# Reordered head pairs, batched value products and a TensorE-held residual in a two-layer streaming encoder step

## The chip, the cores and the metric

The kernel runs on one core of one Trainium2 chip. The metric is the device time of one execution in microseconds (us), from the first to the last instruction of the core plus what lies around them. TensorE appears in the profile as two engines: PE (matmuls) and PEld (loading of the stationary 128 x 128 weights). DVE is VectorE, ACT is ScalarE, POOL is GpSimd, and SP issues most of the DMA transfers.

## The reference, cut to what matters

One inference step of an encoder of two layers, width 1024, over T = 1088 tokens: 1024 new frames of one stream ("prompt") and 64 frames of a running stream ("sample"). All is float32. Layer 0 is a Mamba-2 mixer and a SwiGLU FFN, layer 1 a banded attention and a SwiGLU FFN. The part that the change touches most:

```python
def rmsnorm(x, w):
    return x * lax.rsqrt(jnp.mean(x * x, axis=-1, keepdims=True) + EPS) * w
...
# layer 1: K and V from the residual x, 16 heads of 64
kv = rmsnorm(x, kv_norm_w) @ w_kv
q  = rmsnorm(x, nw[0]) @ attn_w_q
# queries in chunks of 64; a chunk sees itself and the 8 chunks before it
s = einsum('bqhd,bkhd->bhqk', q, k) * 64 ** -0.5 + rel_bias[:, clip(qpos - kpos, -256, 256) + 256]
p = softmax(where(valid, s, -inf))
m = einsum('bhqk,bkhd->bqhd', p, v) @ attn_w_o
# both layers
x = x + rmsnorm(m, nw[1])
x = x + rmsnorm(swiglu(rmsnorm(x, nw[2]), ffn_w_in, ffn_w_out), nw[3])
```

In layer 0, `m` comes from a projection, a causal convolution of four taps with SiLU, a chunked state-space scan and an output projection. K and V of the last 512 prompt tokens and of the sample are outputs too. Sample queries see 512 cached rows of K and V beside their own.

## The kernel before, in words

**Tiling.** Activations lie transposed, 128 features on partitions and tokens along the free axis. The tokens are cut in three *slices* `SL` of 384, 384 and 320, and, where FFN pairs and the output of the attention are concerned, in four quarters `QS` of 256, 256, 288 and 288. For accuracy each matmul operand is split into a high and a low part, and each product is made of three (L415 to L417: high x high, high x low, low x high, in `passes`). One projection *unit* for a slice is 8 x 3 = 24 matmuls into one PSUM bank (`mm`, two banks).

**Order.** TensorE runs in an order written out by hand: the main program issues units, and side tasks are Python generators in a `Stream` (L73). Each matmul adds an estimate of its time to `st.t`; a task yields (cost, delay, condition) and is resumed by `pump` once `st.t` has reached its due time and its condition holds; `wait_for` advances `st.t` by 0.25 a step until its condition is true. All of this happens when the program is built. The chip then runs each engine's queue in order, with semaphores between the engines. The other engines' order follows priorities (`tc.high_priority`; HIP = 3000).

**Weights.** `Weights` (L200) is a ring in the order given by `plan`: a raw buffer (two) filled by a 512 KB DMA on SP's queue (`load`, L224), then `plain` (L243), which makes the high part on ACT (L312) and the low part on DVE (L313) into one of three `hl` buffers. The attention's weights are first scaled on POOL by a norm's weights (L248).

**Layer 0.** The convolution (L716 to L748) takes a projection out of PSUM into `raw`, makes the first tap on ACT (L738) into the tile `cvt` (one buffer), adds three taps on DVE (L740) and applies SiLU on ACT (L744 to L747) into `dst`. L992 sends the low parts of the first weights to POOL (`W.eng = G`). The FFN's first product runs pair by pair (`run_pair`, L1219); the FFN's output projection (L1391 to L1425, matmuls L1405 to L1407) goes slice by slice, with the `end` task (L1311) of each slice behind it: it takes the sum of squares through `rstd` (L443, matmuls L448), broadcasts the reciprocal root (`rb_steps`), multiplies the output by it (L1326 or L1323) and adds the residual x (L1324, L1327). In layer 0 it then makes the split operands `u` for layer 1 and a second sum of squares (L1352), whose broadcast `rb` (`done2` holds ("rb", s)) is multiplied into K, Q and V when they leave PSUM. In layer 1 the last slice's end is the kernel's tail: multiplies on DVE and, for m = 1, 3, 5, on POOL, adds on DVE, one output DMA for each m.

**Attention (L1452 to L1749).** Heads go in pairs j = 0 to 7, one pair to 128 partitions. `evk` (L1506), `evq` (L1526) and `evv` (L1558) take a unit of K, Q or V out of PSUM. `evk` keeps high and low of each head stacked on 128 partitions; `evq` makes for each head `qh` twice (two ACT copies, L1537 and L1538) and `ql` twice (DVE, L1540), so that one product with `qh` and one with `ql` give all terms. `evv` spawns `v_task` (L1545, transposes V) and three `att_task` (L1575), one for each block of 128 queries. A block has three stages, A, B and C, counted in `cur`:

- A: scores of both heads into a tile `S` of two banks (L1610, L1611), then on DVE bias and maximum (L1617), combination of the two banks' maxima (L1622), negation (L1623), on ACT the exponential (L1624), on DVE reciprocal (L1625) and scaling (L1626).
- B: up to five transposes for each head (L1638) into a tile of the same two buffers (`psS`), copies to `pT` on DVE or ACT (L1642, L1644; four buffers).
- C: `pT` with V (L1661, weights 64 wide) into `po`, one of two banks of `ax`, kept through the three blocks of a slice; then a copy `ot` (L1668) and a DMA (L1669) to the DRAM tensor `oscr`.

Block b + 1 may start A once block b - 1 has made B, and B once its own A's scores are due and C of block b - 2 is done. `build_o` (L1681) reads `oscr` back quarter by quarter (L1688) and splits it (L1689, L1690) for the output projection.

The main order (L1700 to L1749): V, K, Q of pair 0 for slices 0 and 1; K of pair 1 for these; a wait for slice 2's norm, ("rb", 2); pair 0's slice 2 as K, Q, V; then for each pair j = 1 to 7 and each slice K, Q, V, each behind a wait that keeps the ring of K and V tiles (`KBUF` = 5, `free_k`, L1676) and of Q tiles (three) from being overrun. The side load of cached K and V rows (`load_side`, L1477) stands in that loop behind a wait for the pair before to be done.

## Time and profile before

Three runs took 3090.6, 3090.92 and 3097.8 us. One more was profiled; where the profile is read below, it is this one.

| what | us |
|---|---|
| median of three runs | 3090.92 |
| the profiled execution's own time | 3083.24 |
| its span, first to last instruction | 3081.1 |
| stretch 0 to 1610 us (layer 0, to near the end of its FFN's output projection) | 1610.0 |
| stretch 1610 to 1700 (the rest of it, first K, V and Q units, slice 2's norm) | 90.0 |
| stretch 1700 to 1792 (first attention blocks) | 92.0 |
| stretch 1792 to 2194.65 (six steady head pairs) | 402.65 |
| stretch 2194.65 to 3081.1 (last pair, output projection, FFN of layer 1) | 886.45 |

The mean clock that TensorE was granted is 0.990 of full speed. The span holds 329 MB of DMA traffic, 107 GB/s on average.

A page of the profile lists for each engine its busy time; groups of instructions by source line ("L313 DVE ..."), with count, busy time, mean length and the idle time ahead of them; and what released an engine from a wait (in the view of the waits a row names the waiting engine and line, "<-" the engine and line that ended the wait, then the idle us in all, the number of waits and the longest). A timeline row has start, duration, engine, line, operation, output <- input, shape and count, and in brackets the idle time ahead of it and its releaser. Matmul durations overlap, since they are pipelined: the pace is read from start to start. A row of the windows view has the stretch, its length, busy time and instruction count of PE, PEld, DVE, ACT and POOL, the granted clock, the DMA engines' share and GB/s.

### The profile page before, as it was taken

How to read it: one execution, taken by the hardware profiler on the slowest of the kernel's cores; microseconds unless marked ns; L12 is line 12 of the kernel's file. 1: busy time of each engine (PE TensorE's matmuls, PEld its weight loads, DVE VectorE, ACT ScalarE, POOL GpSimd, SP SyncE). 2: the span in 40 equal slices, each digit the busy share in tenths (PEclk: the TensorE clock that was granted, in tenths of full speed). 3: DMA queues.
4: the chain of work that ended last, by engine and by line, in shares of the span. 5: the costliest groups of instructions: out<-in, count | busy, mean ns of one | idle time of the engine just before them, and what ended most of it. 6: DMA issues, size and time to landing. Idle time of an engine off the chain costs nothing.

```text
span 3081.1 us, 56781 instructions
## 1 busy us (share of the span) xinstructions
PE 2989.6 (97%) x21761; PEld 2908.2 (94%) x21761; DVE 2117.1 (69%) x4579; ACT 1419.9 (46%) x2512; POOL 880.4 (29%) x1011
## 2 busy tenths in 40 slices
PE   8999999999999999999999899999999999999998
PEld 8899999999999999999999788889898999999997
DVE  8878788796778545574566788887768645575544
ACT  6656565664443222344443454444554332244432
POOL 2333333331344343341223111100054334342112
PEclk9999999999999999999999999999999999999999
DMA  3111111125553222345663121122355222246654
GB/s 118 39 52 51 57 51 59 51 89 151 170 166 107 83 78 74 99 149 176 194 188 123 61 68 60 55 61 62 114 168 166 78 78 76 79 124 183 205 181 132
DMA packets 176511, 329.14 MB, mean 107 GB/s; under 512 B 17360, under 2 KB 124752, under 8 KB 176240
## 3 DMA queue, kind: packets, MB, share of 16 engines
q1 hardware_dynamic: 174448, 319.16, 33.4%
q0 software_dynamic: 1792, 6.36, 1.1%
q8 instruction: 171, 2.80, 0.4%
q14 instruction: 100, 0.82, 0.1%
HBM read 262.85 MB, written 62.60 MB: 106 GB/s over the span
## 4 chain that ended last, share of the span: by engine, by line
PE 81%; DVE 10%; DMA 3%; issue 2%; ACT 2%; POOL 2%; SPq 0%; DVEq 0%; POOLq 0%; ACTq 0%
PE mm L415 8%; PE px L1235 8%; PE px L1236 8%; PE px L1237 8%; PE mm L417 8%; PE mm L416 8%; PE po L1407 5%; PE po L1405 5%; PE po L1406 5%; PE mmx L415 2%; PE mmx L416 2%; PE mmx L417 2%; PE po L1661 2%; PE ptp L1638 2%; DVE hl L313 1%
## 5 line engine op out<-in xcount | busy, mean ns | idle before, releaser
L313 DVE TENSOR_TENSOR hl<-raw,hl 128x1024 fp32r<-128x1024 f32 (+1 forms) x292 | 359.7, 1233 | 313.5 <-ACT hl L312 312.9
L415 PE MATMUL mm<-r,hl 128*128 128x384 f32 (+2 forms) x1664 | 560.3, 337 | 5.9 <-ACT BT L746 4.8
L417 PE MATMUL mm<-r,hl 128*128 128x384 f32 (+2 forms) x1664 | 540.2, 325 | 0.6 <-DVE hl L313 0.6
L416 PE MATMUL mm<-r,hl 128*128 128x384 f32 (+2 forms) x1664 | 539.8, 324 | 0.0
L312 ACT CAST hl<-raw 128x1024 fp32r<-128x1024 f32 (+1 forms) x295 | 297.8, 1014 | 302.1 <-PE po L1407 98.7
L1236 PE MATMUL px<-r,hl 128*128 128x288 f32 (+1 forms) x1192 | 350.1, 294 | 0.0
L415 PEld LDWEIGHTS mm<-r,hl 128*128 128x128 f32 x1664 | 316.2, 190 | 14.6 <-issue 6.7
L441 POOL TENSOR_TENSOR ssum<-ssum,sq 128x256 f32<-128x256 f32 (+3 forms) x153 | 166.0, 1091 | 540.8 <-ACT sq L440 537.6
L416 PEld LDWEIGHTS mm<-r,hl 128*128 128x128 f32 x1664 | 316.5, 190 | 0.4
L417 PEld LDWEIGHTS mm<-r,hl 128*128 128x128 f32 x1664 | 315.6, 190 | 1.0 <-DVE hl L313 1.0
L1235 PE MATMUL px<-r,hl 128*128 128x288 f32 x1056 | 311.7, 295 | 4.1 <-DVE u L1250 3.9
L1237 PE MATMUL px<-r,hl 128*128 128x288 f32 x1056 | 311.2, 295 | 0.0
L1237 PE MATMUL px<-rx,hl 128*128 128x256 f32 x816 | 229.1, 281 | 6.5 <-DVE hl L313 6.5
L1235 PE MATMUL px<-rx,hl 128*128 128x256 f32 x816 | 230.0, 282 | 0.0
L1236 PEld LDWEIGHTS px<-r,hl 128*128 128x128 f32 x1192 | 224.0, 188 | 0.1
L1406 PE MATMUL po<-rx,hl 128*128 128x384 f32 (+1 forms) x640 | 208.0, 325 | 0.0
L1235 PEld LDWEIGHTS px<-r,hl 128*128 128x128 f32 x1056 | 198.7, 188 | 5.7 <-DVE u L1250 5.7
L1405 PE MATMUL po<-rx,hl 128*128 128x384 f32 (+1 forms) x608 | 199.6, 328 | 0.0
L1237 PEld LDWEIGHTS px<-r,hl 128*128 128x128 f32 x1056 | 198.4, 188 | 0.0
L1407 PE MATMUL po<-rx,hl 128*128 128x384 f32 (+1 forms) x608 | 198.0, 326 | 0.3 <-DVE hl L313 0.3
L1236 PE MATMUL px<-rx,hl 128*128 128x256 f32 x680 | 191.1, 281 | 0.0
L262 POOL TENSOR_TENSOR tt<-raw 128x512 f32<-128x512 f32 x44 | 60.0, 1363 | 396.9 <-DMA raw<-in_w_f_dram 207.8
(348 smaller groups left out, 8147.4 us busy)
## 6 DMA issues: line engine op xcount, KB each, us to landing
raw<-in_w_f_dram SPq DMA_DIRECT2D x204, 512.0 KB, 3.8
raw<-in_w_in_dram SPq DMA_DIRECT2D x40, 512.0 KB, 3.6
raw<-in_w_f_dram SPq DMA_DIRECT2D x48, 384.0 KB, 3.2
sg<-hscr SPq DMA_DIRECT2D x88, 192.0 KB, 3.6
raw<-in_w_so_dram SPq DMA_DIRECT2D x32, 512.0 KB, 3.9
raw<-in_w_kv_dram SPq DMA_DIRECT2D x18, 512.0 KB, 3.6
raw<-in_w_o_dram SPq DMA_DIRECT2D x16, 512.0 KB, 3.8
sg<-hscr SPq DMA_DIRECT2D x44, 160.0 KB, 3.6
```

The source lines that it names most:

```text
L312: self.nc.scalar.copy(h, v)
L313: (eng or self.eng or self.nc.vector).tensor_tensor(lo, v, h, op=ALU.subtract)
L415: PE.matmul(ps[:, :n], h_, xh, start=(first and i == 0), stop=False)
L416: PE.matmul(ps[:, :n], h_, xl, start=False, stop=False)
L417: PE.matmul(ps[:, :n], l_, xh, start=False, stop=(last and i == nk - 1))
L441: (eng or G).tensor_tensor(ssum[:, :n], ssum[:, :n], q[:, :n], op=ALU.add)
L1235: PE.matmul(ps, wh, ah[:, k, :], start=(k == 0), stop=False)
L1236: PE.matmul(ps, wh, al[:, k, :], start=False, stop=False)
L1237: PE.matmul(ps, wl, ah[:, k, :], start=False, stop=(k == 3))
L1405: PE.matmul(ps[:, :n], wh, xh, start=(k == 0), stop=False)
L1406: PE.matmul(ps[:, :n], wh, xl, start=False, stop=False)
L1407: PE.matmul(ps[:, :n], wl, xh, start=False, stop=(k == FT - 1))
```

## The change

The edits, in the order of the diff:

1. Scaled weights (attention): eight scaled ACT copies and eight DVE multiply-subtracts of 128 x 128 in place of POOL's scaling, ACT's cast and DVE's subtraction (`scaled`).
2. `rstd` with two sums keeps them in separate PSUM columns and adds them on DVE.
3. The convolution works in `dst`; the tile `cvt` is gone. `W.eng = G` is gone.
4. The tail: x goes into PSUM on TensorE (product with the identity) for m = 0 to 5, DVE multiplies y, TensorE adds it to x in PSUM, and ACT copies the sum out; m = 6 and 7 are added on DVE. Some due times change.
5. The second norm of layer 0's last slice is issued once K's product for slice 2 has been ("k2").
6. During the FFN output projections the weight splits have priority 1500 (`W.pri`).
7. Attention order: for each pair and slice K, V, Q instead of K, Q, V; `att_task` is spawned by `evq`, 5.0 behind it, and `v_task` 3.0 behind `evv`. The side load is a task of its own. All three evacuations have priority 3000. Q tiles have two buffers.
8. `ql`'s second copy comes from the first by a DMA within SBUF on SP's queue.
9. The softmax computes the negative scores' minimum, chained from the first bank to the second, so that combination and negation go; it and the copies of B have priority 1000.
10. C is held: `values` runs a slice's three blocks together ahead of the first transposes of the next slice (for the last pair, behind its own slice's last block). `pT` has six buffers.
11. The last pair's outputs of slices 0 and 1 stay on chip for `build_o`, which reads three pairs rather than four from DRAM for that half.
12. Around slice 2 of pair 0: the products of K and V are issued ahead of the wait for ("rb", 2), and their evacuations behind it; then V of pair 1 for slices 0 and 1, then Q of pair 0 for slice 2.

```diff
-EP_W, ER_W, EQ_W = (9.4, 9.4, 5.0), (8.9, 8.9, 4.5), (11.0, 11.0, 11.0)
+EP_W, ER_W, EQ_W = (9.4, 9.4, 2.2), (8.9, 8.9, 3.3), (11.0, 11.0)
-LDP, ENP = 1500, (0, 0, 1500)
+LDP, ENP, ATP = 1500, (0, 0, 1500), 1000
...
         if it.get("kscale") is not None:
-            v3 = r.rearrange("p (k m) -> p k m", m=P)
-            self.nc.gpsimd.tensor_tensor(v3, v3, it["kscale"].unsqueeze(2).to_broadcast([P, KD, P]), op=ALU.mult)
-        self.part(it, "w", None, r[:, :n])
+            self.scaled(it, r)
+        else:
+            self.part(it, "w", None, r[:, :n])
...
+    def scaled(self, it, r):
+
+        self.used.append(self.hl)
+        t = self.hl.get()
+        for k in range(KD):
+            sl, c = slice(k * P, (k + 1) * P), it["kscale"][:, k:k + 1]
+            self.nc.scalar.activation(t[:, 0, sl], r[:, sl], AF.Copy, scale=c)
+        for k in range(KD):
+            sl, c = slice(k * P, (k + 1) * P), it["kscale"][:, k:k + 1]
+            self.nc.vector.scalar_tensor_tensor(t[:, 1, sl], r[:, sl], c, t[:, 0, sl], op0=ALU.mult, op1=ALU.subtract)
+        it["w"] = t[:, 0, :], t[:, 1, :]
...
-        for i in range(nb):
-            for j, t in enumerate(ts):
-                PE.matmul(
-                    sp[:, i:i + 1], t[:, i * P:(i + 1) * P], ones[:, 0:1], start=(j == 0), stop=(j == len(ts) - 1)
-                )
+        for j, t in enumerate(ts):
+            for i in range(nb):
+                c = 4 * j + i
+                PE.matmul(sp[:, c:c + 1], t[:, i * P:(i + 1) * P], ones[:, 0:1], start=True, stop=True)
...
+            if more is not None:
+                V.scalar_tensor_tensor(a, sp[:, 4:4 + nb], inv, a, op0=ALU.mult, op1=ALU.add)
...
-                cvt = sb2.tile([P, 384], F32, tag="cvt", bufs=1, name="cvt")
+
                 cw = C_CW + ct * 4
-                A.activation(cvt[:, :w_], raw[:, 0:w_], AF.Identity, bias=col(C_CB + ct), scale=col(cw))
+                A.activation(dst[:, :w_], raw[:, 0:w_], AF.Identity, bias=col(C_CB + ct), scale=col(cw))
                 for k in range(1, 4):
                     V.scalar_tensor_tensor(
-                        cvt[:, :w_], raw[:, k:k + w_], col(cw + k), cvt[:, :w_], op0=ALU.mult, op1=ALU.add
+                        dst[:, :w_], raw[:, k:k + w_], col(cw + k), dst[:, :w_], op0=ALU.mult, op1=ALU.add
                     )
                 if s < 2:
-                    A.activation(dst[:, :384], cvt[:, :384], AF.Silu)
+                    A.activation(dst[:, :384], dst[:, :384], AF.Silu)
                 else:
-                    A.activation(dst[:, 0:256], cvt[:, :256], AF.Silu)
-                    A.activation(dst[:, 256:320], cvt[:, 259:323], AF.Silu)
+                    A.activation(dst[:, 0:256], dst[:, :256], AF.Silu)
+                    A.activation(dst[:, 256:320], dst[:, 259:323], AF.Silu)
...
-        W.eng = G
...
+                if s == 2 and more is None:
+                    yield 0, EP_W[2]
+                steps = rb_steps(ss, n, out, ER_W[s], more=more)
...
+                    xps = {}
+                    def hold(ms):
+                        for m in ms:
+                            xps[m] = mm("xp") if m > 3 else px.tile([P, 512], F32, tag="mm", name="xp")
+                            PE.matmul(xps[m][:, :n], ident, xs[m][0], start=True, stop=False)
+
+                    yield next(steps)
+                    hold(range(4))
+                    yield next(steps)
+                    yield next(steps)
+                    hold((4, 5))
+                    for m in range(KD):
+                        ym = y[:, m, :n]
+                        V.scalar_tensor_tensor(ym, ym, col(cpost2 + m), out[0], op0=ALU.mult, op1=ALU.mult)
+                        if m in xps:
+                            PE.matmul(xps[m][:, :n], ident, ym, start=False, stop=True)
+                            A.copy(ym, xps[m][:, :n])
+                        else:
+                            V.tensor_tensor(ym, ym, xs[m][0], op=ALU.add)
+                        nc.sync.dma_start(xout[:, m, o:o + n], ym)
...
-                yield 0, EQ_W[s]
+                yield (0, EQ_W[s]) if s < 2 else (0, 0, lambda: "k2" in done2)
...
+            W.pri = LDP
...
-    W.plan(W_V[0], W_K[0], W_Q[0], W_K[1], W_V[0])
-    for j in range(1, 8):
-        W.plan(W_K[j], W_Q[j], W_V[j])
+    W.plan(W_V[0], W_K[0], W_Q[0], W_K[1], W_V[0], W_V[1], W_K[1], W_Q[1])
+    for j in range(2, 8):
+        W.plan(W_K[j], W_V[j], W_Q[j])
...
+        def side_task(j):
+
+            yield 0, 0, lambda: cur["C"] >= 9 * j
+            load_side(j)
...
-                Q = [[sb2.tile([P, 384], F32R, tag=f"Q{x}{e}", bufs=3, name=f"Q{x}{e}") for x in "hl"] for e in range(2)]
+                Q = [[sb2.tile([P, 384], F32R, tag=f"Q{x}{e}", bufs=2, name=f"Q{x}{e}") for x in "hl"] for e in range(2)]
...
-                    for x in range(2):
-                        V.tensor_tensor(ql[H2[x], :n], qf[H2[e], :n], qh[H2[e], :n], op=ALU.subtract)
+                    V.tensor_tensor(ql[H2[e], :n], qf[H2[e], :n], qh[H2[e], :n], op=ALU.subtract)
+                    nc.sync.dma_start(ql[H2[1 - e], :n].bitcast(F32), ql[H2[e], :n].bitcast(F32))
+                for i in range(3):
+                    st.spawn(att_task(j, 3 * s + i), 5.0 + 0.1 * i)
...
-                st.spawn(v_task(j, s, vt), 1.5 if j else 5.0)
-                for i in range(3):
-                    st.spawn(att_task(j, 3 * s + i), 2.0 + 0.1 * i)
+                st.spawn(v_task(j, s, vt), 3.0 if j else 5.0)
...
+            yield 0, 0, lambda: (
+                late and cur["A"] == seqn and cur["B"] >= seqn - 1 and st.t >= cur["t"] and s in d["K"] and s in d["Q"] and (b < 8 or "Ck" in d)
+            )
...
+                low = TOP
+                with tc.high_priority(ATP):
+                    for pi, (f0, f1) in enumerate([(0, split)] + ([(split, w_)] if split < w_ else [])):
+                        V.tensor_tensor_reduce(
+                            out=sc[:L, f0:f1], in0=sp[:L, pi, :f1 - f0], in1=brev[:, f0:f1],
+                            scale=-1.0, scalar=low, op0=ALU.add, op1=ALU.min, accum_out=mx[:L, pi:pi + 1],
+                        )
+                        low = mx[:L, pi:pi + 1]
+                    A.activation(sc[:L, :w_], sc[:L, :w_], AF.Exp, bias=low, scale=-1.0, accum_out=mx[:L, 3:4])
+                    V.reciprocal(mx[:L, 3:4], mx[:L, 3:4])
+                    V.tensor_scalar(sc[:L, :w_], sc[:L, :w_], mx[:L, 3:4], None, op0=ALU.mult)
...
-            yield 1.1 * w_ / 640, AT_W1, lambda: cur["B"] == seqn and cur["C"] >= seqn - 1 and st.t >= cur["t"]
+            yield 1.1 * w_ / 640, AT_W1, lambda: (
+                cur["B"] == seqn and st.t >= cur["t"] and (i > 0 or not held or held[0][:2] in v_done)
+            )
+            cost = values(held) if i == 0 else 0
...
-                pT = late["sb3"].tile([P, 5, P], F32, tag="pT", bufs=4, name="pT")
+                pT = late["sb3"].tile([P, 5, P], F32, tag="pT", bufs=6, name="pT")
...
+            held.append((j, s, i, L, nkt, w_, k0, PTs))
+            yield cost, 0
+            if (j, s) == (7, 2) or (j == 7 and i == 2):
+                yield 0, AT_W2, lambda: (j, s) in v_done
+                yield values(held), 0
+        def values(blocks):
...
+            while blocks:
+                j, s, i, L, nkt, w_, k0, PTs = blocks.pop(0)
+                d = kqv[j]
...
+                    ot = late["sb1"].tile([P, 384], F32, tag=f"o7{s}" if j == 7 and s < 2 else "ot", name="ot")
+                    with tc.high_priority(HIP if j == 7 else 0):
+                        A.copy(ot[:, :n], po[:, :n])
+                    nc.sync.dma_start(od_[:, j, o:o + n], ot[:, :n])
+                    if j == 7 and s < 2:
+                        last_o[s] = ot
+                    att_done.append((j, s))
+                cur["C"] += 1
...
+        def free_q(q, stage):
 
             j_, s_ = divmod(q - KBUF, 3)
-            return j_ < 0 or cur["C"] > 9 * j_ + (6, 7, 8)[s_]
+            return j_ < 0 or cur[stage] > 9 * j_ + (6, 7, 8)[s_]
 
...
+                    nk = 4 - (kh and q < 2)
...
+                if nk == 3:
+                    yield 0, 0, lambda: all((7, s) in att_done for s in of)
+                    for s in of:
+                        a, b = max(o, SL[s][0]), min(o + n, SL[s][0] + SL[s][1])
+                        src = last_o[s][:, a - SL[s][0]:b - SL[s][0]]
+                        with tc.high_priority(HIP):
+                            A.copy(h[:, 3, a - o:b - o], src)
+                            V.tensor_tensor(l_[:, 3, a - o:b - o], src, h[:, 3, a - o:b - o], op=ALU.subtract)
...
-        st.wait_for(lambda: ("rb", 2) in done)
...
+        wv = W.get()
+        n2, kv2 = SL[2][1], []
+        for w in (wk, wv):
+            ps = mm("mm")
+            passes(ps, w, lambda k: u[2][k], [(k, k) for k in range(KD)], n2, parts=4)
+            kv2.append(ps)
+            done.append("k2")
+            st.pump()
+        st.wait_for(lambda: ("rb", 2) in done)
+        for ps, e in zip(kv2, (evk, evv)):
+            e(0)(2, ps)
             W.put()
+            st.pump()
+        wv = W.get()
+        units(wv, 1, evv, (0, 1))
+        st.wait_for(lambda: cur["A"] >= 3)
+        units(wq, 0, evq, (2,))
+        W.put()
         for j in range(1, 8):
             if j > 1:
                 load_pair(j)
             load_bias(j)
...
+            ws = [W.get(), W.get() if j > 1 else wv, W.get()]
+            evs = [evk, evv, evq]
+            for s, i in [(s, i) for s in range(NSL) for i in range(3) if j > 1 or s == 2 or i == 2]:
+                q = 3 * j + s
+                if (s, i) == (2, 0):
+                    st.spawn(side_task(j))
+                st.wait_for(lambda: cur["A"] >= 3 * (q - 1) if i == 2 else free_q(q, "AC"[i]))
+                units(ws[i], j, evs[i], (s,))
...
+        st.wait_for(lambda: cur["C"] == 8 * NCH and 1 in uo)
```

130 lines of the change are left out of this document (51 added, 79 removed).

## The prediction, made before the result was known

> **What bounds the kernel now.** I read the page's busy times first, then the stretches of the windows view, then who waited for whom inside a stretch, and last the timeline at the waits.
>
> ```profile
> span 3081.1 us, 56781 instructions
> ...
> PE 2989.6 (97%) x21761; PEld 2908.2 (94%) x21761; DVE 2117.1 (69%) x4579; ACT 1419.9 (46%) x2512; POOL 880.4 (29%) x1011
> ```
>
> TensorE is busy for 2989.6 of 3081.1 us, and the change takes none of its products away. Only 91.5 us of idle time, the time at a low clock, and what TensorE loses between kinds of matmul can be won. Where the idle time lies (columns: length, then busy us with instruction counts of PE, PEld, DVE, ACT, POOL, the granted clock, DMA share, GB/s):
>
> ```profile
> 0.00:150.00 150.00, 134.77 (x864) 124.59 (x864) 123.69 (x305) 96.62 (x166) 40.83 (x89) 0.98 0.23 77
> 1595.00:1610.00 15.00, 11.48 (x57) 10.95 (x57) 11.10 (x10) 8.65 (x16) 10.10 (x8) 0.77 0.61 190
> 1672.00:1693.00 21.00, 14.64 (x70) 14.07 (x70) 16.45 (x32) 7.87 (x17) 6.07 (x10) 0.76 0.30 96
> 1700.00:1792.00 92.00, 81.34 (x610) 72.43 (x609) 75.61 (x237) 45.18 (x103) 13.99 (x11) 0.96 0.20 63
> 1792.00:2194.65 402.65, 386.18 (x2998) 356.14 (x2998) 322.46 (x1001) 195.88 (x435) 29.68 (x35) 1.00 0.20 62
> 1763.53:1766.94 3.41, 1.57 (x11) 1.08 (x10) 2.02 (x4) 2.70 (x5) 0.00 (x0) 1.00 0.02 9
> 1766.94:1770.35 3.41, 2.95 (x12) 2.76 (x13) 3.28 (x13) 2.06 (x6) 0.00 (x0) 0.50 0.15 50
> 3063.00:3081.10 18.10, 3.96 (x22) 2.85 (x20) 10.05 (x23) 0.86 (x2) 2.99 (x3) 0.62 0.21 72
> ```
>
> Idle time in these: start 15.2 us; end of layer 0's FFN 3.5; slice 2's norm ahead of the attention 6.4; first attention blocks 10.7; the six steady head pairs 16.5; the tail 14.1. That is 66 of the 91.5 us, all in places that the change touches. A wait costs more than itself: from 1763.53 PE worked 1.57 of 3.41 us, and the next 3.41 us had a clock of 0.50.
>
> **Part by part.** *AV products by slice.* Each block's AV product (L1661) is its own batch, 8 pairs x 9 blocks = 72. The change holds them and runs a slice's three together, 24 batches.
>
> ```profile
> 1848.66 0.34 PE L1610 MATMUL S<-K,Qh 128*128 128x384 f32 x1
> 1848.84 0.33 PE L1611 MATMUL S<-K,Ql 128*128 128x384 f32 x1
> 1849.10 1.09 PE L1661 MATMUL po<-pT,Vn 128*64 128x128 f32 x16
> 1850.13 0.42 PE L415 MATMUL mm<-r,hl 128*128 128x320 f32 x1
> 1850.38 0.31 PE L416 MATMUL mm<-r,hl 128*128 128x320 f32 x1
> 1850.53 0.31 PE L417 MATMUL mm<-r,hl 128*128 128x320 f32 x1
> ```
>
> From start to start a 384-column product takes 0.18 us; ahead of the AV batch (its weights are 64 wide) it takes 0.26: 0.08 lost. A 320-column product takes 0.15, so 128 columns take 0.06; 16 make 0.94, and 1.03 pass: 0.09 lost. The first projection after it takes 0.25 in place of 0.15: 0.10 lost. So 0.27 us a batch, times 48 batches fewer, **-13**. Where only transposes follow, less is lost: 0.15 or 7 us is my low end. The weight loader's own idle time ahead of these batches bounds it above:
>
> ```profile
> PEld po L1661 <- issue: 8.8, 35, 0.3
> ```
>
> 8.8/35 = 0.25 us on the way in and no more than that out: 0.5 x 48 = 24 us.
>
> *The steady pairs' waits.*
>
> ```profile
> PE ptp L1638 <- DVE mx L1617: 9.8, 6, 2.6
> PE S L1610 <- ACT pT L1642: 5.9, 6, 1.0
> ```
>
> ```profile
> 1847.65 0.15 DVE L1625 RECIPROCAL mx<-mx 128x1 f32<-128x1 f32 x1
> 1847.73 0.46 DVE L1540 TENSOR_TENSOR Ql<-qf,Qh 64x320 fp32r<-64x320 f32 x1
> ...
> 1848.66 3.10 DVE L1540 TENSOR_TENSOR Ql<-qf,Qh 64x320 fp32r<-64x320 f32 x3
> ```
>
> ```profile
> 1845.35 2.03 POOL L248 TENSOR_TENSOR raw<-raw,pcs 128x1024 f32<-128x1024 f32 x1 [32.05 <-DMA raw<-in_w_kv_dram]
> 1849.42 1.99 POOL L248 TENSOR_TENSOR raw<-raw,pcs 128x1024 f32<-128x1024 f32 x1 [2.04 <-DMA raw<-in_w_kv_dram]
> ```
>
> ```profile
> 1852.74 1.44 PE L1638 MATMUL ptp<-ident,sc 128*128 128x128 f32 x8 [1.47 <-DVE mx L1617]
> ```
>
> One Ql split takes 0.46 us alone; three take 3.10 while POOL scales a weight. The score reductions behind them in DVE's queue come late, both score buffers stay full, and PE waits 1.47 us for one. The change takes L248 off POOL, halves the Ql splits (six of 0.46, 2.8 us a pair), drops two kinds of 128x1 operation (18 negations and ten maxima a pair, at the 0.15 of the reciprocal: 4 us), and puts the softmax at priority 1000, ahead of weight splits. It adds eight multiply-subtracts of 128x128 in place of one subtraction:
>
> ```profile
> L313 DVE TENSOR_TENSOR hl<-raw,hl 128x1024 fp32r<-128x1024 f32 x18 | 22.0, 1223 | 3.3 <-ACT hl L312 3.1
> ```
>
> ```profile
> 23.40 0.29 DVE L990 TENSOR_TENSOR dtw<-dtr,dtw 128x128 fp32r<-128x128 f32 x1
> ```
>
> ```profile
> 1705.98 0.25 ACT L1642 COPY pT<-ptp 128x128 f32<-128x128 f32 x1
> ```
>
> 8 x 0.29 = 2.3 us against 1.22, three weights a pair: +3.3 us on DVE; eight casts of 0.25 = 2.0 us on ACT where one of about 1 us stood. Net, DVE loses some 3.5 us of work a pair and all the time behind POOL; ACT (49% busy) gains 3. Both lie beside TensorE: a weight buffer is refilled while the pair's other units and blocks run, so this costs nothing unless a refill comes over 10 us late. Of the 15.7 us I take **-12**; the ends are 0 and -16.5. A longer hold of the pT tiles is covered by six buffers for four, and `po` no longer keeps one of the two `ax` banks through three blocks. Moving the side load out of the main loop lets it wait without holding the units behind it.
>
> *Ql's second half by DMA.* This is the added wait. evq now issues two transfers of 96 KB for each slice on SP's queue, each waiting there for its DVE split; weight loads and K/V outputs queue behind for that time, and these have slack. The scores wait for the landing. No row shows a transfer within SBUF; the nearest are
>
> ```profile
> hscr<-u SPq DMA_DIRECT2D x34, 128.0 KB, 1.7
> ```
>
> ```profile
> cr<-in_ckT_dram SPq DMA_DIRECT2D x16, 128.0 KB, 2.6
> ```
>
> Head 1's path after its unit: multiply, three casts and a split on 64 partitions at about 0.46-0.5 each, 2.4 us with idle engines, then 1.7 to 2.6: 4.1 to 5.0 us, with DVE 80% and ACT 49% busy around it. Its first scores are placed 5.0 us of counted work behind evq. So PE waits between 0 and 1.1 us for each of 24 slices if the engines are prompt, and up to 3 if they are not. I take 0.3: **+7** (ends 0 and +72).
>
> *Slice 2's products beside its norm.*
>
> ```profile
> PE nst L448 <- POOL ssum L1352: 4.0, 1, 4.0
> PE nst L448 <- DVE ssum L1352: 2.4, 1, 2.4
> ```
>
> The norm's sums are now placed behind K's slice 2, so the unfinished Q and K units and that product come first; V's 3.5 us (24 x 0.15) cover the chain behind the sums, and two V units of pair 1 follow. The 6.4 us idle and up to 0.24 x 14.6 = 3.5 us of low clock can go; about 2 stays where the broadcast waits for DVE: **-7.5** (ends -3 and -9.9).
>
> *Weight splits at priority 1500 in the output projections.*
>
> ```profile
> PE po L1405 <- ACT hl L312: 2.5, 1, 2.5
> PE po L1407 <- DVE hl L313: 1.0, 1, 1.0
> ```
>
> 3.5 us idle and 0.23 x 11.5 = 2.6 of low clock. POOL's squares still slow DVE there: **-4** (ends 0 and -6).
>
> *First attention blocks.* The 10.7 us have the same causes as the steady waits, but V of pair 1 has moved ahead, so fewer projection pieces lie between the blocks: **-4** (ends +6 and -12).
>
> *Start.* The weight split on POOL and the single cvt tile go.
>
> ```profile
> PE mm L415 <- ACT BT L746: 4.8, 1, 4.8
> ```
>
> The split comes back on DVE at 1.2 us each, so part of this: **-3** (ends 0 and -7).
>
> *Tail.*
>
> ```profile
> 3070.09 4.30 DVE L1326 SCALAR_TENSOR_TENSOR y<-y,pcs,rb 128x320 f32<-128x320 f32 x5 [1.98 <-ACT rb L479]
> 3074.32 1.00 DVE L1324 SCALAR_TENSOR_TENSOR y<-y,pcs,r 128x320 f32<-128x320 f32 x2
> 3075.24 2.08 DVE L1327 TENSOR_TENSOR y<-y,r 128x320 f32<-128x320 f32 x5
> 3077.25 0.54 DVE L1324 SCALAR_TENSOR_TENSOR y<-y,pcs,r 128x320 f32<-128x320 f32 x1
> ```
>
> 7.7 us of DVE, the first five at 0.86 beside POOL. After: eight multiplies and two adds at 0.42 = 4.2; the other adds go through TensorE and ACT beside them, with a last copy behind: **-3** (ends 0 and -4.5). The last pair's outputs kept on chip skip a DRAM trip; its wait is in the 15.7 us, and I count nothing more.
>
> Sum: -13 -12 +7 -7.5 -4 -4 -3 -3 = -39.5. The profiled execution took 3083.24 us (span 3081.1), so it would take 3044; the runs shown have a median of 3090.92, 7.7 above it, so I forecast **3051**.
>
> One rule of the Trainium skill speaks against part of this. "TensorE: Matmul & The Clock Gate", section "What's actually happening", has the clock fall to half after at least one idle window of about 3.4 us. Read strictly, waits of 1.8 to 2.5 us would cost no clock, 5 us of the clock terms would not be there, and the sum would be -34.5, 3056. The trace disagrees: the window with 1.57 us of work in 3.41 was followed by 0.50.
>
> **The rivals.** (1) *All waits go.* The ql transfer is in time (-7), the steady waits vanish (-4.5), the first blocks and the small terms reach their ends (-15): 3025. For it: all steady waits end at DVE or ACT work that POOL delays. (2) *The attention keeps its waits.* With PE's order fixed at build time, new places wait where old ones went: +16 on the forecast, 3067. For it: DVE stays above 70% busy, and the score buffers remain two. (3) *ql comes late* (slower than before). The mechanism is the transfer behind head 1's split. Without it the change is worth 46.5 us; 46.5/24 = 1.9 us a slice breaks even, about 3090. At 3 us a slice it costs 72, and as the clock falls after such waits, some 4-5 us more in all: about 3120. For it: DVE's and ACT's queues were 80% and 49% busy, and a split is seen to take 3.10 for three. Against it: POOL's L248 was what stretched it.
>
> **How the numbers follow.** Forecast 3051 (3037 to 3062): 0.46. Rival 1: 0.22. Rival 2: 0.19. Rival 3 near break-even: 0.05; well past it: 0.08. The range 3020 to 3079 leaves out the last two. Faster by over 0.3% (9.3 us; about what a measurement of this kernel tells from no change) is 0.46 + 0.22 + 0.19 = 0.87, same 0.05, slower 0.08.
>
> **What would show it.** Steady pairs of about 63 us in place of 67.1 (402.65/6), 24 stretches of L1661 rather than 72; no wait for the score buffers of over 1 us in them; at the start of a slice a wait of S for ql of under 0.5 us; PE idle under 3 us in slice 2's norm, with the clock at 1.00; the multiplies of the tail at 0.42 each. The forecast is wrong if S waits 1 us or more for ql's landing in most slices, or if weights of the attention come late because their sixteen small operations have no priority.

## The result, and the profile after

The changed kernel took 3046.7 us (median of four runs, 3044.14 to 3050.39) beside 3091.86 for the kernel before: a ratio of 0.9853, 95% interval 0.9837 to 0.9868, or 45 us less. A second measurement, beside runs of before of its own, gave 0.9859 (0.9842 to 0.9876). The forecast was 3051. The profiled execution took 3046.85, its span is 3045.2. That is 35.9 us under the span of the profile of before, and not 45, since the profiled execution of before (3083.24) was faster than its median.

Page of the changed kernel: span and busy times.

```profile
span 3045.2 us, 56936 instructions
...
PE 2981.5 (98%) x21785; PEld 2913.9 (96%) x21785; DVE 2075.4 (68%) x4498; ACT 1463.6 (48%) x2703; POOL 816.2 (27%) x975
```

TensorE's idle time fell from 91.5 to 63.7 us and its busy time by 8.1; switching between kinds of matmul and time at a low clock show as busy time, so what they gave lies in the second number. To see where, both traces are cut at the starts of TensorE instructions that both kernels have (the last cut is at an end): the first product `yo` of the state-space scan, the first FFN product `px` of layer 1, the first and last output-projection product `po` of both FFNs, and the last value product of the attention. Each stretch up to the tail holds the same number of matmuls in both. (The second profile is that of `changed_again` below.)

| stretch, us | before | changed | changed, second profile |
|---|---|---|---|
| start to first `yo` | 98.60 | 103.15 | 105.50 |
| to first `po` of layer 0 | 1273.94 | 1274.80 | 1275.20 |
| to last `po` of layer 0 | 273.62 | 269.39 | 269.15 |
| to last value product (the attention) | 568.78 | 528.08 | 527.47 |
| to first `px` of layer 1 | 164.37 | 169.80 | 165.03 |
| to first `po` of layer 1 | 419.69 | 421.72 | 420.40 |
| to last `po` of layer 1 | 265.13 | 264.84 | 264.68 |
| to the end (tail) | 17.00 | 13.38 | 13.39 |

The attention gave 41 us, the first output projection 4, the tail 3.6; the start got 4.6 to 6.9 longer. The 5.4 us lost behind the attention in the first profile were that execution's: the second has 0.7.

Windows of the changed kernel (length, busy us and counts of PE, PEld, DVE, ACT, POOL, clock, DMA share, GB/s): the first attention blocks and five further pairs.

```profile
1687.43:1800.37 112.94, 108.48 (x855) 102.45 (x854) 90.86 (x300) 70.15 (x180) 0.65 (x5) 1.00 0.23 70
1800.37:2116.22 315.85, 311.45 (x2496) 297.18 (x2496) 245.07 (x767) 187.13 (x468) 3.04 (x20) 1.00 0.26 77
```

Of 112.94 us in the first blocks PE idles 4.5 (10.7 of 92.0 before), of 315.85 us in the steady pairs 4.4. Between the scores on cached rows of four successive pairs lie 253.04 us, 63.3 a pair, where before had 267.66, 66.9. Who PE waited for in those four pairs, before and then changed (total us, times, longest):

```profile
PE ptp L1638 <- DVE mx L1617: 5.7, 4, 2.3
PE S L1610 <- ACT pT L1642: 4.0, 4, 1.0
```

```profile
PE S L1654 <- DVE pT L1691: 2.2, 7, 0.4
PE ptp L1686 <- DVE mx L1664: 1.5, 4, 0.8
```

The same two places still wait, 3.7 us in place of 9.7, and none longer than 0.8. No row names `Ql`, the low part of the queries whose second half now comes by DMA.

For the whole attention stretch I added up, from TensorE's starts, the waits of over 0.15 us, the time at a clock of 0.50, and the start-to-start times of the products at which TensorE goes to or from a value batch:

| attention stretch | us | waits | half clock | switches |
|---|---|---|---|---|
| before | 568.8 | 32.6 | 20.5 | 143, 31.0 us |
| changed | 528.1 | 12.5 | 3.4 | 51, 11.1 us |
| changed, second profile | 527.5 | 13.4 | 0 | 51, 11.1 us |

Waits give 19 to 20 us. At half a clock a 384-column product starts every 0.32 us in place of 0.17, so I take it to cost half its time: 17.1 to 20.5 us less of it, 8.5 to 10. What is left of the 41, about 12, I put down to the switching; the second experiment tests that.

### The profile page after: what moved, and what is told of

It reads as the page before. It is cut to its first block, busy times and chain, and to the rows that moved or that the text cites. A ratio compares the mean times of both kernels' runs of the same rounds, so it can differ in the third digit from the quotient of the medians.

```text
span 3045.2 us, 56936 instructions
## 1 busy us (share of the span) xinstructions
PE 2981.5 (98%) x21785; PEld 2913.9 (96%) x21785; DVE 2075.4 (68%) x4498; ACT 1463.6 (48%) x2703; POOL 816.2 (27%) x975
## 5 line engine op out<-in xcount | busy, mean ns | idle before, releaser
L313 DVE TENSOR_TENSOR hl<-raw,hl 128x1024 fp32r<-128x1024 f32 (+1 forms) x269 | 332.0, 1235 | 299.7 <-ACT hl L312 298.6
L312 ACT CAST hl<-raw 128x1024 fp32r<-128x1024 f32 (+1 forms) x269 | 270.7, 1010 | 263.8 <-DMA raw<-in_w_f_dram 98.8
L427 PEld LDWEIGHTS mm<-r,hl 128*128 128x128 f32 x1664 | 315.5, 190 | 11.5 <-issue 5.1
```

The source lines that it names most:

```text
L312: self.nc.scalar.copy(h, v)
L313: (eng or self.eng or self.nc.vector).tensor_tensor(lo, v, h, op=ALU.subtract)
L427: PE.matmul(ps[:, :n], h_, xh, start=(first and i == 0), stop=False)
```

## The experiments

Each is the changed kernel with one edit, whose main lines are shown ("..." stands for lines left out), and nothing else. Ratios are to before on the same chip, most with an interval of 0.0015 to either side (4.6 us), so they seldom separate two kernels of this table. The stretches carry the verdicts: in the six profiles whose edit, if any, lies outside the attention, it takes 525.6 to 528.1 us. Each stretch is of one execution, and for value products by block and for the last pair through DRAM that was the slowest of four.

| kernel | ratio (95%) | attention, us | waits | half clock |
|---|---|---|---|---|
| changed_again | 0.9859 (0.9842 to 0.9876) | 527.5 | 13.4 | 0 |
| av_by_block | 0.9910 (0.9895 to 0.9924) | 548.3 | 14.6 | 17.1 |
| pool_scale | 0.9877 (0.9862 to 0.9893) | 540.9 | 20.1 | 13.7 |
| last_from_dram | 0.9888 (0.9873 to 0.9904) | 536.3 | 19.8 | 6.8 |
| softmax_prio0 | 0.9878 (0.9862 to 0.9895) | 535.1 | 18.3 | 3.4 |
| ql_by_dve | 0.9873 (0.9858 to 0.9888) | 534.2 | 19.5 | 0 |
| norm_first | 0.9874 (0.9859 to 0.9889) | 533.8 | 15.9 | 10.2 |
| split_prio0 | 0.9880 (0.9863 to 0.9898) | 527.1 | 12.2 | 3.4 |
| softmax_ops | 0.9855 (0.9840 to 0.9869) | 525.7 | 14.2 | 0 |
| conv_and_split | 0.9835 (0.9820 to 0.9850) | 525.7 | 12.0 | 0 |
| conv_tile | 0.9847 (0.9832 to 0.9862) | 526.1 | 12.4 | 0 |
| first_split_pool | 0.9843 (0.9827 to 0.9859) | 525.6 | 12.1 | 0 |

**The same kernel again.**

> The changed kernel as it is, beside the runs of before on this chip, so that the single edits have a second measure to stand against. Expected: ratio to before 0.984 to 0.987; the stretch from the last output-projection matmul of layer 0 to the last value product 525 to 529 us (528.1 in the first profile, 568.8 in before); first yo 103 to 105.5; the 5.6 us by which the first profile was longer between the last value product and the first px (169.8 for 164.4) is not seen again, if it was that one execution's.

As expected in all points, though first `yo`, at 105.50, lies at the very end of its range.

**Value products by block.**

```diff
-                cur["B"] == seqn and st.t >= cur["t"] and (i > 0 or not held or held[0][:2] in v_done)
+                cur["B"] == seqn and cur["C"] >= seqn - 1 and st.t >= cur["t"]
...
-            cost = values(held) if i == 0 else 0
+            cost = 0
...
-            if (j, s) == (7, 2) or (j == 7 and i == 2):
-                yield 0, AT_W2, lambda: (j, s) in v_done
-                yield values(held), 0
+            yield 0, AT_W2, lambda: cur["C"] == seqn and (j, s) in v_done
+            yield values([held.pop(0)]), 0
```

> The changed kernel with each block's value product run by itself, 72 batches for 24, as before. Theory: a batch costs TensorE 0.27 us of switching (0.08 in, 0.19 out), so 48 more cost 13 us (7 to 24): about 3060, steady pairs 1.6 us longer (63.3 to 64.9 us), and the pitch into and out of the value batches in the attention rises from 11 us to about 31 us with 144 switches for about 52. Rival: the gain came from fewer waits, since the held products give softmax time; then the switches account for less than half of what is lost and new waits of S or ptp of over 0.5 us a pair show up. Second rival: order is free, within 4 us of 3047.

The stretch is 20.5 us longer than the mean of the two changed profiles (some 17 us by the ratios). 143 switches take 31.1 us in place of 11.1 for 51; waits add 1.6 us, half clock 15.4 us, that is 7.7; 11.2 remain, 0.23 us for each of the 48 batches. So the switching costs about what the theory said, and more comes with it: a lower clock, likely from waits such as these (the attention's, this kernel):

```profile
PE ptp L1686 <- DVE mx L1664: 5.7, 4, 3.2
PE S L1655 <- DMA Ql<-Ql: 2.3, 2, 2.1
```

Switching is over half of the loss, so the rival falls as the whole reason and stands as a part. The second row is the wait that the prediction feared: one of 2.1 us and one of 0.2.

The four steady pairs show the price without waits or low clock. By block and then changed:

```profile
1869.66:2127.15 257.49, 256.67 (x1997) 237.52 (x1996) 191.27 (x612) 145.87 (x372) 2.34 (x16) 1.00 0.23 71
```

```profile
1863.18:2116.22 253.04, 249.32 (x1997) 237.76 (x1997) 196.26 (x614) 149.96 (x375) 2.46 (x16) 1.00 0.26 78
```

By block TensorE has no wait of over 0.15 us in them, and they are still 4.5 us longer (5.2 against the second changed profile, 252.29); with the changed kernel's 3.6 to 3.8 us of waits that makes 8 to 9 us for 24 more batches, 0.34 to 0.37 us each. The pairs of before give the same: 14.6 us longer, 6.0 of them waits, 0.36 a batch. Here the switching is all of the loss.

**POOL's scaling back.**

```diff
         if it.get("kscale") is not None:
-            self.scaled(it, r)
-        else:
-            self.part(it, "w", None, r[:, :n])
+            v3 = r.rearrange("p (k m) -> p k m", m=P)
+            self.nc.gpsimd.tensor_tensor(v3, v3, it["kscale"].unsqueeze(2).to_broadcast([P, KD, P]), op=ALU.mult)
+        self.part(it, "w", None, r[:, :n])
```

> The changed kernel with POOL's scaling of the attention weights back (then one cast on ACT and one subtraction on DVE), nothing else. Theory: DVE operations that run beside POOL's 2 us scaling are stretched (0.46 us to 1.0 us for a Ql split in before), so the steady waits come back in good part: +4 to +12 us, 3051 to 3059, with the mean Ql split above 0.60 us (0.53 in the changed kernel, 0.70 in before) and idle waits of PE in the four pairs from the second cached-row score on above 5 us (3.7 in the changed kernel, 9.7 in before). Rival: the waits went because of the softmax's priority and its fewer operations; then within 3 us of 3047 although the Ql splits are longer. Rival below: since DVE has 3.3 us and ACT some 3 us a pair less to do, up to 4 us faster.

DVE's groups in the same four pairs, changed and then with POOL's scaling (busy us, mean ns, idle ahead):

```profile
L1671 DVE TENSOR_SCALAR sc<-sc,mx 128x640 f32<-128x640 f32 (+5 forms) x72 | 34.0, 472 | 1.5
L325 DVE SCALAR_TENSOR_TENSOR hl<-raw,pcs,hl 128x128 fp32r<-128x128 f32 x96 | 29.9, 345 | 0.8
...
L1581 DVE TENSOR_TENSOR Ql<-qf,Qh 64x384 fp32r<-64x384 f32 (+1 forms) x24 | 12.7, 530 | 6.4 <-ACT Qh L1579 6.1
```

```profile
L1671 DVE TENSOR_SCALAR sc<-sc,mx 128x640 f32<-128x640 f32 (+5 forms) x72 | 40.6, 568 | 1.8
...
L1581 DVE TENSOR_TENSOR Ql<-qf,Qh 64x384 fp32r<-64x384 f32 (+1 forms) x24 | 16.2, 675 | 6.4 <-ACT Qh L1579 6.1
L313 DVE TENSOR_TENSOR hl<-raw,hl 128x1024 fp32r<-128x1024 f32 x12 | 14.7, 1221 | 2.5 <-ACT hl L312 2.5
```

POOL saves DVE 15.2 us of splits in four pairs (29.9 against 14.7), but two operations that run beside it stretch, 530 to 675 ns and 472 to 568 ns. Form by form, the splits of 64x320 go from 484 to 919 ns and the scalings of 128x256 from 354 to 900, while the scalings of 128x640 stay at 550. So DVE is busy for about as long either way, 196.3 us changed and 197.4 with POOL; what differs is which operations are slow: the scalings are part of the softmax, and the splits stand ahead of score reductions in DVE's queue. In the four pairs PE's waits rise from 3.7 to 6.1 us, as expected, and the pairs take 3.4 us more. The attention as a whole is 13 us longer, with 7 us more of waits and 12 of half clock, and most of that, 8 to 9 us, lies ahead of the first pair's cached rows, where the waits are others: 3.3 us for slice 2's norm, 2.4 for K's evacuation, 2.0 for one landing of `Ql`. The kernel lost about 6.5 us by the ratios, within what was expected, though the intervals overlap. The theory holds for the steady pairs; it is not what makes up most of the 13 us.

**ql by DVE, softmax without priority, softmax with the old operations.**

```diff
-                    nc.sync.dma_start(ql[H2[1 - e], :n].bitcast(F32), ql[H2[e], :n].bitcast(F32))
+                    V.tensor_tensor(ql[H2[1 - e], :n], qf[H2[e], :n], qh[H2[e], :n], op=ALU.subtract)
...
-LDP, ENP, ATP = 1500, (0, 0, 1500), 1000
+LDP, ENP, ATP = 1500, (0, 0, 1500), 0
...
-                            scale=-1.0, scalar=low, op0=ALU.add, op1=ALU.min, accum_out=mx[:L, pi:pi + 1],
+                            scale=1.0, scalar=0.0, op0=ALU.add, op1=ALU.max, accum_out=mx[:L, pi:pi + 1],
...
+                    if split < w_:
+                        V.tensor_tensor(mx[:L, 0:1], mx[:L, 0:1], mx[:L, 1:2], op=ALU.max)
+                    V.tensor_scalar(mx[:L, 2:3], mx[:L, 0:1], -1.0, None, op0=ALU.mult)
```

> The changed kernel with ql's second half by DVE subtraction again in place of the transfer within SBUF. The changed kernel shows no wait of the scores for ql. Theory (the transfer is hidden and DVE has room): within 4 us of the changed kernel, steady pairs 63.0 to 64.0 us. Rival (the DVE time it saved is part of the gain, since the score reductions stand behind the splits): 24 x 2 x 0.53 = 25 us more on DVE make it 4 to 12 us slower, with waits of ptp for L1664 and of S for L1691 of over 8 us in all in place of 8.2 between them in the whole attention. Rival of the prediction (transfers cost 0.3 us a slice): 7 us faster.

> The changed kernel with the softmax and its copies without priority (ATP = 0). Theory (the waits went because POOL no longer stretches DVE, and priority orders DVE's queue a little better): +3 to +10 us, waits of the attention up from 12.5 to 15 to 22 us. Rival (priority does nothing, since the queue is short): within 3 us. Rival (priority is the main cause): +15 us or more.

> The changed kernel with the softmax's old operations (maximum for each bank, their combination, a negation), at the new priority. Theory (DVE's work ahead of the exponential is what the attention waits for): 18 negations and ten combinations a pair at 0.15 = 4 us more on DVE a pair, 34 us in all, cost 4 to 9 us, as the 25 us of the ql splits cost 6 to 8; the attention's waits rise from 12.5 to 16 to 21 us. Rival (only long operations matter): within 3 us, since each adds 0.15 us to a chain.

The first two are 6.4 and 7.3 us longer in the attention, with 6.5 and 5.3 us more of waits, so priority is worth what its theory said. ql by DVE, the attention's waits (2.8 and 5.2 us in the changed kernel):

```profile
PE ptp L1686 <- DVE mx L1664: 6.2, 8, 0.9
PE S L1654 <- DVE pT L1691: 5.5, 18, 0.5
```

So the transfer is a gain of some 6 us and not a cost of 7: the scores never wait for it in the changed kernel, and DVE is rid of 25 us ahead of its score reductions. The theory that DVE had room falls; its rival holds. The third edit, the old operations, changes nothing (525.7 us): its theory falls. Its DVE groups, against 37.2 and 17.0 us for L1664's two forms in the changed kernel:

```profile
L1664 DVE CUSTOM_DVE_ANT_0 sc<-S,bias 128x384 f32<-128x384 f32 (+4 forms) x112 | 50.1, 478 | 7.0 <-PE S L1655 5.3 <-POOL bias L1540 1.3 <-issue 0.3
...
L1670 DVE TENSOR_SCALAR mx<-mx 128x1 f32<-128x1 f32 (+1 forms) x72 | 10.5, 148 | 0.8
...
L1669 DVE TENSOR_TENSOR mx<-mx 128x1 f32<-128x1 f32 (+1 forms) x40 | 6.1, 153 | 0.2
```

The small operations (the two lower rows) cost 16.6 us in four pairs and the chained reduction 4.1 more than the plain one, so 12.5 us go from DVE and TensorE sees none of it. Why 12.5 us here are free and the ql splits' are not was not separated; the splits come three or four in a row when a slice's queries arrive, the small ones one by one, which is an argument and not a measurement.

**Slice 2's norm as before.**

```diff
-                yield (0, EQ_W[s]) if s < 2 else (0, 0, lambda: "k2" in done2)
+                yield 0, 11.0
...
         st.wait_for(lambda: 2 in done)
+        st.wait_for(lambda: ("rb", 2) in done)
...
-        st.wait_for(lambda: ("rb", 2) in done)
         for ps, e in zip(kv2, (evk, evv)):
```

> The changed kernel with slice 2's norm placed as before (sums 11.0 behind, and the wait for its broadcast ahead of K's and V's products of slice 2); V of pair 1 still follows. Theory: PE idle for the norm is back at about 6.4 us and the half clock with it (10.2 us of half clock before, 3.4 changed), so +5 to +8 us; the stretch from the last output-projection matmul of layer 0 to the first score is 4 to 7 us longer than the changed kernel's 40.1. Rival: within 2 us, since the units that stand there (pair 1's) cover the norm anyway.

From the last `po` to the first score: 47.8 us before, 40.1 and 38.5 changed, 45.3 here. The theory's size holds (5.2 to 6.8 us), with POOL's wait back, at 3.2 in place of 4.0; but all waits up to the first score are 3.6 us (2.0 changed) and not the 6.4 of before; time at half clock there is 6.8 us (3.4 and 0 changed):

```profile
PE nst L461 <- POOL ssum L1386: 3.2, 1, 3.2
```

**Weight splits without priority in the output projections.** Edit: `W.pri = LDP` becomes `W.pri = 0`.

> The changed kernel with W.pri = 0 in the FFN output projections. Theory: the stretch from first to last matmul of layer 0's output projection, 269.4 to 270.1 us in the changed kernel and its variants and 273.6 in before, is back at 273 to 274.5, and layer 1's is longer by about 1 (263.6 to 264.8 changed, 265.1 before): +4 to +5 us. Rival: the 4 us come from the rest of the change (other releases at the start of the stretch); then it stays at 269 to 270.5.

First to last `po` of layer 0: 273.3 us, as expected; the wait for the cast is back. Here, and then in the changed kernel's second profile:

```profile
PE po L1441 <- ACT hl L312: 2.5, 1, 2.5
PE po L1443 <- DVE hl L313: 1.2, 2, 1.0
```

```profile
PE po L1443 <- DVE hl L313: 1.5, 2, 1.2
PE po L1441 <- ACT hl L312: 0.8, 1, 0.8
```

In layer 1 it is 265.3, where the other kernels of the table lie between 263.6 and 264.9: too little to tell from no change.

**The last pair through DRAM.** Edit: `nk = 4 - (kh and q < 2)` becomes `nk = 4`.

> The changed kernel with the last pair's outputs read back through DRAM like the others. The prediction counted nothing for this beyond the waits. Theory: the trip (copy, write of 1.8 us, read of 4.7 us, split) is covered by the last blocks for quarter 0 only in part, so +1 to +5 us, between Ck6 and the first FFN product of layer 1. Rival: covered in full, within 2 us and no new wait of mm for L1756 or L1757 (the copy and the split). Rival above: over 6 us, since the wait also costs clock.

The attention grows by 8.5 us, 8.1 of them between the cached-row scores of the last two pairs, with the largest wait of the stretch:

```profile
PE mm L427 <- ACT r L1761: 5.3, 1, 5.3
```

The rival above 6 us holds. The kernel before has no row of this kind at that place, though it took the same trip: the wait comes with the rest of the change, and keeping the outputs on chip stops it. Which part of the change uncovers the trip (the faster attention, or the values held to the end of the slice) was not tried.

**The start.** Three kernels: with the first edit (the three taps and SiLU then work in `cvt` too), with the second (POOL up to the end of the first units), with both.

```diff
+                cvt = sb2.tile([P, 384], F32, tag="cvt", bufs=1, name="cvt")
...
-                A.activation(dst[:, :w_], raw[:, 0:w_], AF.Identity, bias=col(C_CB + ct), scale=col(cw))
+                A.activation(cvt[:, :w_], raw[:, 0:w_], AF.Identity, bias=col(C_CB + ct), scale=col(cw))
...
+        W.eng = G
```

> The changed kernel with the convolution's single tile cvt put back, nothing else. Theory: with one tile, the convolution's multiply-adds of the second and third output came late and left DVE free for the norm's chain of 128x1 operations (40.2 to 42.6 us in before); without it they stand between the chain's steps (40.2 to 45.2 us), TensorE waits 2.31 us for the broadcast and then has a half clock from 45.42. So with the tile back that wait is under 0.5 us and the first yo matmul starts 3.5 to 4.5 us earlier than in the changed kernel (103.15): 98.6 to 99.7, as before (98.60); the kernel takes about 3043 in place of 3047. Rival: the weight splits that moved from POOL to DVE delay the chain; then the wait at 42 us stays over 1.5 us and first yo stays within 1 us of 103.15.

> The changed kernel with the first weights' low parts on POOL again (W.eng = G), nothing else. Theory (the missing conv tile costs the start its 4.5 us): first yo stays within 1 us of the changed kernel's 103.15 and the 2.31 us wait for the norm's broadcast stays over 1.5 us. Rival (the splits on DVE cost it): the wait falls under 0.5 us and first yo is back at 98.6 to 100.

> The changed kernel with both edits of the start undone: the convolution's tile cvt and the first weights' low parts on POOL; the rest as changed. Theory after the two single runs (with the tile alone the wait for the norm's broadcast went, but TensorE waited 7.1 us for BT; with POOL alone that wait went to 3.4 us in two, but the broadcast's 2.3 us stayed): the two need each other, so with both first yo is back at 98.6 (98.1 to 99.6, against 102.3 to 105.5 with one or none), and the kernel gains 4 to 5 us on the changed one: ratio to before about 0.984. Rival: the start's 4.5 us come from somewhere else (the norm's sums, the order of loads); then first yo stays above 102.

What stretched the norm's chain, DVE's timeline before and then changed (start, length, operation):

```profile
40.29 0.29 DVE L455 TENSOR_SCALAR nv<-nv 128x3 int32<-128x3 int32 x2
40.49 0.29 DVE L458 TENSOR_TENSOR nv<-nv 128x3 f32<-128x3 f32 x2
```

```profile
40.27 0.16 DVE L468 TENSOR_SCALAR nv<-nv 128x3 int32<-128x3 int32 x1
40.34 0.61 DVE L753 SCALAR_TENSOR_TENSOR BT<-craw,pcs,BT 128x384 f32<-128x384 f32 x1
40.87 0.15 DVE L471 TENSOR_TENSOR nv<-nv 128x3 f32<-128x3 f32 x1
40.94 0.16 DVE L468 TENSOR_SCALAR nv<-nv 128x3 int32<-128x3 int32 x1
41.01 0.61 DVE L753 SCALAR_TENSOR_TENSOR CT<-craw,pcs,CT 128x384 f32<-128x384 f32 x1
41.54 0.17 DVE L472 TENSOR_TENSOR nv<-nv 128x3 f32<-128x3 f32 x1
```

Before, two norms' steps follow each other every 0.2 us; changed, steps wait out one 0.6 us step of a convolution that the single tile had held back (with the tile back they follow each other every 0.2 us again). PE's waits up to 97 us, changed, with the tile back, with POOL back, with both:

```profile
PE mm L427 <- DVE craw L713: 4.5, 1, 4.5
...
PE nbp L488 <- DVE nr L476: 2.3, 1, 2.3
```

```profile
PE mm L427 <- ACT BT L760: 7.1, 1, 7.1
```

```profile
PE nbp L488 <- DVE nr L476: 2.3, 1, 2.3
PE mm L427 <- ACT CT L760: 1.8, 1, 1.8
...
PE mm L427 <- DVE craw L713: 1.6, 1, 1.6
```

```profile
PE mm L427 <- ACT BT L759: 4.8, 1, 4.8
```

The first expectation was half right: the tile takes the wait for the broadcast away, but first `yo` stays at 104.87, since the wait for BT grows to 7.1. POOL alone gives 102.31 and keeps the broadcast's wait. With both edits undone the waits of over 2 us are those of before, and first `yo` comes at 101.50, not at the 98.6 expected: 11.5 us at half clock in place of 6.8 account, by estimate, for 2.3 of the 2.9 us. First `yo` alone is a poor measure, since ten profiles with the changed start have it at 103.15 to 108.04, with 9.9 to 21.6 us at half clock. All waits up to it are steadier: 12.9 us before, 15.4 and 15.5 changed, 16.4 with the tile, 14.7 with POOL, 13.3 with both. With both undone the kernel has the lowest ratio measured, 0.9835 (3038.64 us); its interval overlaps those of the changed kernel, so against that one the gain is likely and not proved. POOL alone is close to it, 0.9843 (3038.17 us on another chip).

## Why the prediction came out right, point by point

The forecast of 3051 is 4 us above the measured 3046.7, but two steps of the sum had the wrong sign, in opposite directions, and one was half its size. So the nearness of the number is partly luck: with the terms as measured below the sum is about -41 in place of -39.5, although single terms are off by up to 10 us.

- *AV products by slice*, -13: about 12 in the balance of the stretches, 11.2 in the experiment. Right: 0.23 us a batch over the whole attention and some 0.35 in the steady pairs, for the 0.27 read from one place of the trace.
- *Steady pairs' waits*, -12: 9.7 us of waits in four pairs became 3.7, which makes 9 for six. Somewhat mis-sized. The cause named, DVE stretched beside POOL, holds; of the other three causes named, priority and fewer ql splits count and the 128x1 operations do not.
- *Ql's second half by DMA*, +7: wrong in sign. The transfer lands 1.9 to 3.7 us after its issue; the median, 2.0, is within the 1.7 to 2.6 read from other transfers, the longest above. The step that failed is "Its first scores are placed 5.0 us of counted work behind evq": in the built program that delay could be 0 or 2 with TensorE's order unchanged, because a block waits for the blocks ahead of it. (By the prediction's own figures, a path of 4.1 to 5.0 us behind 5.0 us of work, prompt engines leave no wait; its "between 0 and 1.1 us" doesn't follow from them.) From the second issue of a slice to the slice's first product with ql pass 2.6 to 5.9 us (12.9 in the first slice), and in 20 of 24 slices over 2 us of that lie behind the landing. Where the attention slowed (value products by block, POOL's scaling), one slice in each did wait 2 us, so the cover is thin.

Changed kernel, issues of this transfer (count, KB, median us to landing):

```profile
Ql<-Ql SPq DMA_DIRECT2D x32, 96.0 KB, 2.1
...
Ql<-Ql SPq DMA_DIRECT2D x16, 80.0 KB, 2.0
```

- *Slice 2's products beside its norm*, -7.5: -7.7 and -9.3; 2 us of wait stay, as put there, though for V's evacuation and not for the broadcast.
- *Weight splits at priority 1500*, -4: -4.2 and -4.5 in layer 0, under 0.5 in layer 1.
- *First attention blocks*, -4: mis-sized. Waits fell from 10.3 to 4.4 us and 6.8 us of half clock went: 9 us, from windows of 92 and 113 us that don't hold the same work, so an estimate. They had the same causes as the steady waits, and the prediction took a smaller share of them for no measured reason.
- *Start*, -3: wrong in sign, +4.6 to +6.9. The step "The weight split on POOL and the single cvt tile go" counted the wait that ended at BT and not what the tile held back: convolution steps, now free to run between the norm's. The tile and POOL's splits both have a part in it: only with both back do the waits come near those of before. A stall that goes needs the question what runs earlier in its place.
- *Tail*, -3: -3.6. The multiplies run at 0.47 us each where five took 0.86:

```profile
3036.85 3.79 DVE L1347 SCALAR_TENSOR_TENSOR y<-y,pcs,rb 128x320 f32<-128x320 f32 x8 [1.36 <-ACT rb L492]
3037.46 3.50 PE L1349 MATMUL xp<-y,ident 128*128 128x320 f32 x12
3038.30 3.12 ACT L1350 COPY y<-xp 128x320 f32<-128x320 f32 x6 [1.48 <-PE xp L1349]
```

- *Last pair kept on chip*, nothing: right as a difference to before, but not for free: without it 8.5 us would have been given back.
- Rivals: the first (3025) named the right direction for the attention, where nearly all waits of over 1 us did go. (Its "-15" is added up short: the ends that it names make -17.9, and 3022.) The second and third did not happen: of the third, no score of the changed kernel waits for the landing.

## What to carry to other kernels

Work that an idle engine takes over is not free when it slows the busy engine's operations beside it: measure the busy engine's mean, form by form, with and without. A buffer that serializes work may be what lets a chain of short dependent operations run closely; before it goes, look at what stands behind it in the in-order queue. And a faster or reordered stretch can uncover a transfer that was hidden: look at the next one behind it.

## What was not expected of the hardware

The same wait costs clock in one execution and none in the next. In both profiles of the changed kernel PE waits 1.96 us for V's evacuation. Windows of the clock's own 3.41 us, first profile and then second:

```profile
1670.17:1673.58 3.41, 1.54 (x9) 1.54 (x10) 3.38 (x7) 2.53 (x9) 2.00 (x2) 1.00 0.13 43
1673.58:1676.99 3.41, 3.41 (x13) 3.31 (x12) 3.35 (x11) 1.02 (x2) 0.26 (x2) 0.50 0.73 191
```

```profile
1670.57:1673.98 3.41, 1.99 (x12) 1.67 (x10) 3.35 (x6) 3.41 (x12) 2.41 (x3) 1.00 0.00 0
1673.98:1677.39 3.41, 2.87 (x17) 2.83 (x18) 3.35 (x9) 1.21 (x5) 0.74 (x1) 1.00 0.32 107
```

The first wait lies within one window, 1.54 of 3.41 us are busy, and the next has 0.50. The second is split over two windows, 1.99 and 2.87 us busy, and the clock stays. But how busy PE is in a window does not settle it alone. In the same second execution, in layer 0:

```profile
687.51:690.92 3.41, 2.93 (x22) 2.80 (x23) 3.41 (x15) 2.69 (x6) 0.00 (x0) 1.00 0.60 203
690.92:694.34 3.42, 3.42 (x18) 3.42 (x18) 3.42 (x16) 1.58 (x5) 0.00 (x0) 0.50 0.53 162
960.60:964.01 3.41, 1.54 (x14) 1.34 (x12) 3.38 (x3) 0.00 (x0) 0.00 (x0) 1.00 0.82 306
964.01:967.43 3.42, 1.66 (x14) 1.66 (x15) 3.42 (x4) 2.58 (x4) 1.89 (x2) 1.00 0.16 49
```

A window with 2.93 us of work is followed by 0.50, one with 1.54 us is not. What the clock goes by stays open here; that the split of the wait over two windows saved it is a reading and not shown. That a window need not be idle for the clock to fall speaks again for the trace and against the strict reading of the Trainium skill weighed in the prediction ("TensorE: Matmul & The Clock Gate", section "What's actually happening"). That the window runs freely and does not start with the kernel, which the same section of the Trainium skill states, fits these rows: counted from the span's start, the windows of the second execution lie 0.40 us later than those of the first. That is likely also why the start of the ten profiles with the changed start differs by up to 5 us.
